# Stick-breaking scores in a hybrid attention layer: two query blocks on the two halves of the array's rows

## The chip, the cores and the metric

The kernel runs on one core of a Trainium2 chip. The core has TensorE (PE in the profile; its weight loads have a row of their own, PEld), VectorE (DVE), ScalarE (ACT), GpSimd (POOL), and SyncE (SP), whose queue issues nearly all of this kernel's DMAs. The metric is the device time of one execution in microseconds. All times below are microseconds unless marked ns.

## The reference, cut to what matters

The layer has two attention branches. The change is in the first, stick-breaking attention with 8 heads of 64 dimensions, 2048 real positions and 16 meta positions:

```python
for blk in range(L // BLOCK):                       # 128 queries at a time
    z = einsum('bqhd,bkhd->bhqk', q[:, q0:end], k[:, :end]) * scale
    mask = (s[None, :] < t[:, None]) & valid[None, :end]
    log_beta = log_sigmoid(z)
    log_1m = where(mask, log_beta - z, 0.0)
    rev = cumsum(log_1m, axis=3, reverse=True)
    suffix = concatenate([rev[..., 1:], zeros_like(rev[..., :1])], -1)
    w = where(mask, exp(log_beta + suffix), 0.0)
    outs.append(einsum('bhqk,bkhd->bqhd', w, v[:, :end]))
```

Everything is float32. Around it stand an RMS norm, one large input projection, the sliding-window branch, gates, two branch projections, an output projection and a final norm.

## The kernel before, in words

**Precision.** TensorE multiplies in a reduced float32 format here, so each float32 operand is split into a high part and a low part. A projection takes three products (high·high, low·high, high·low); these are the three matmuls at line 454 (`gemm`).

**Order of positions.** Sequences are reversed, so the suffix product of the reference becomes a running product, and each query block looks at keys to its right. The sequence is cut into four groups `g` of 512 positions. The program runs in two halves, first groups 2 and 3, then 0 and 1. In each half come projections, the sliding-window stage, and then the stick-breaking stage `stick(groups, bp)`.

**The stick-breaking stage.** A step is `(h, g, n, j)`: head `h`, query group `g`, key chunk `n`, query block `j` of four. Query block `j` against chunk `n` covers 512 keys that start on the block's own diagonal. In the last chunk the keys run out, and blocks 0 to 3 cover 512, 400, 272 and 144 columns, the last 16 of them the meta keys. Block 0 has no room for these 16 in its bank and puts them into another bank, `zm`.

- `row` (from line 899) makes the scores of a step: two matmuls at line 916 into one of two banks `z`. The contraction runs over all 128 rows of the array: the key tile `kt` holds the high keys of the head in rows 0 to 63 and the low keys in rows 64 to 127; `q1` holds high over low queries, `q2` low over high. Thus `q1` against `kt` gives high·high + low·low, and `q2` gives low·high + high·low. Line 918 does the same for the 16 meta columns. ScalarE then writes the sigmoid (line 920) into a row buffer, and VectorE runs the product scan over it (line 930; in the first half GpSimd masks the diagonal block before it, line 925).
- `turn` transposes four 128x128 pieces of rows that are 5 or 6 steps old (`LT`) into one of two banks `t` (line 941); `evac_split` takes them out as a high part on ScalarE (line 119) and a low part on VectorE (line 120).
- `values` multiplies these by the values (line 967), two steps after their `turn`.

`load_kv` and `load_q` fetch the keys, values and queries of a head over SP's queue. The key tile has two buffers, the row buffer twelve.

**Order of the work.** The order on TensorE is written out by hand: `weave` runs one step of three matmuls of a gate projection (line 454), and then as much of the stick-breaking generator as the costs that it yields allow. The generator yields estimates in us, 0.45 for the two score matmuls, 0.43 for a `turn`, 0.43 for a `values`. On the other engines and on SP's queue a planner decides the order beforehand; on the chip each engine runs its own list in order.

One more place matters as a comparison: `meta_cols` (line 475) transposes a tile of 16 rows, so that its matmul uses only a strip of the array's rows. It happens a few times in the first 320 us.

Of the kernel before, what the change touches and what calls it, by code (L numbers as in the profile page):

```python
# [7 lines left out]
F32 = mybir.dt.float32  # L8
# [8 lines left out]
P = 128  # L17
# [31 lines left out]
def tile_kernel(ctx, tc, x, xt, meta, metat, gain, w_in, w_sb, w_sw, w_out, sinks, fgain,  # L49
# [8 lines left out]
    def DMA(dst, src):  # L58
        nc.sync.dma_start(*(t.bitcast(F32) if t.dtype == F32R else t for t in (dst, src)))
# [788 lines left out]
    def stick(groups, bp):  # L848
        kt, vc = {}, {}
        rows_of = {}  # L850
        lt = LT[groups[0] == 0]
        KW = ((4 - groups[0]) * GT + P)
        for tag, shape, n in (("q1", [P, GT], 2), ("q2", [P, GT], 2), ("v", [P, 4, P], 5), ("wh", [P, GT], 3), ("wl", [P, GT], 3),
                              ("k", [P, KW], 2)):
# [16 lines left out]
        def load_kv(h, g):  # L871

            p, a = divmod(h, 2)
            r = slice(64 * a, 64 * a + 64)
            if h not in kt:
                kt[h] = bp.tile([P, KW], F32R, tag="k", name="kt", bufs=2)
            for c in range(g, 4):
                if (h, c) in vc:
                    continue
                c0 = (c - groups[0]) * GT  # L880
                cs = slice(c0, c0 + GT + (NM if c == 3 else 0))
                DMA(kt[h][0:64, cs], kd[p][c][0][r])
                DMA(kt[h][64:128, cs], kd[p][c][1][r])
                v = vc[h, c] = bp.tile([P, 4, P], F32R, tag="v", name="vc", bufs=5)
                DMA(v, vd[p][c][a])

# [9 lines left out]

        state = {}

        def row(h, g, n, j):

            if n == j == 0:
                load_kv(h, g)
                state[h, g] = {"q": load_q(h, g), "last": {}}
            st = state[h, g]
            last = st["last"]
            b0 = 4 * (g + n) + j
            nb = min(4, NB - b0)
            end = b0 + nb == NB
            w = nb * P + (NM if end and nb < 4 else 0)
            k0 = (b0 - 4 * groups[0]) * P  # L910
            own = end and nb == 4
            z = ps("z")
            zm = ps("zm") if own else None
            for t, qt in enumerate(st["q"]):
                lq = qt[:, j * P:(j + 1) * P]
                T.matmul(z[:, :w], lhsT=lq, rhs=kt[h][:, k0:k0 + w], start=t == 0, stop=t == 1)  # L916
                if own:
                    T.matmul(zm[:, :NM], lhsT=lq, rhs=kt[h][:, k0 + w:k0 + w + NM], start=t == 0, stop=t == 1)
            r = bp.tile([P, RW], F32, tag="row", name="row", bufs=12)
            A.activation(r[:, :w], z[:, :w], AF.Sigmoid, scale=-1.0)  # L920
            if own:
                A.activation(r[:, w:w + NM], zm[:, :NM], AF.Sigmoid, scale=-1.0)
                w += NM
            if n == 0 and mask is None:
                G.affine_select(out=r[:, :P], in_=r[:, :P], pattern=[[1, P]], compare_op=ALU.is_ge,  # L925
                                fill=1.0, base=-1, channel_multiplier=-1)
            if n == 0 and mask is not None:
                V.tensor_tensor_scan(r[:, :w], r[:, :w], mask[:, :w], 1.0, op0=ALU.mult, op1=ALU.max)
            else:
                V.tensor_tensor_scan(r[:, :w], r[:, :w], r[:, :w], last[j] if n else 1.0, op0=ALU.mult, op1=ALU.min)  # L930
            last[j] = r[:, w - 1:w]
            rows_of[h, g, n, j] = r
# [45 lines left out]
        turned = []  # L978
        for s in range(n + lt + 3):
            if s < n:  # L980
                row(*steps[s])
                yield 0.45 if s >= lt else 1.31
            t = s - lt
            if 0 <= t < n:
                turn(*steps[t])
                turned.append(s)
                yield 0.43
                if sum(steps[t][1:3]) == steps[t][3] == 3:
                    turn_meta(*steps[t][:2])
# [331 lines left out]
    for half, groups in enumerate(halves):  # L1321
# [168 lines left out]
```

## Time and profile before

| | |
|---|---|
| time, median of 3 runs | 2111.91 (2111.11 to 2116.18) |
| the profiled execution's own time | 2112.16 |
| its span | 2110.4 |
| PE busy | 2094.4 (99%) |
| PEld busy | 1755.2 (83%) |
| DVE busy | 1479.1 (70%) |
| ACT busy | 1058.8 (50%) |
| POOL busy | 300.1 (14%) |
| score matmuls, line 916, first to last start | 374.2 to 1599.5, in two stretches |

In a row of the timeline the first two numbers are the start and the duration; for a merged row (x2, x4) the duration covers all of them. Matmuls are pipelined, so a matmul's duration is longer than the distance to the next start; what a matmul costs is read from the distance between starts. A group row gives busy time, mean ns of one, then the engine's idle time just before the group and what ended it.

### The profile page before, as it was taken

Reading aid. Unit: us, or ns where it says so; the run is one execution under the profiler, and the core shown is the slowest. Engines: PE = TensorE matmul, PEld = TensorE weight load, DVE = VectorE, ACT = ScalarE, POOL = GpSimd, SP = SyncE. Lnnn points to the kernel's source line nnn. Section 1 sums busy time; section 2 is a strip of 40 time slices with the busy share of each in tenths; the row PEclk is TensorE's granted clock in tenths of the full one; section 3 lists DMA queues with packets and bytes.
Section 4 is the critical chain, followed back from the end, with each engine's and each line's share of the span. In section 5 each row is a group of like instructions: output and inputs, shape, how many; then the busy total and the mean of one; then the engine's idle time right before and its main releaser. Section 6 shows DMA issues by size and latency. Waiting matters only on the chain.

```text
span 2110.4 us, 30845 instructions
## 1 busy us (share of the span) xinstructions
PE 2094.4 (99%) x10695; PEld 1755.2 (83%) x10695; DVE 1479.1 (70%) x2375; ACT 1058.8 (50%) x2438; POOL 300.1 (14%) x484
## 2 busy tenths in 40 slices
PE   9999999999999999999999999999999999999998
PEld 7888888888878888888888888888888888788887
DVE  7897986888878554887738888877774456564553
ACT  6677774555646335777735555555553202221131
POOL 2133444211000000232310000000000232000000
PEclk9999999999999999999999999999999999999999
DMA  9955545766449674435455344343424996568532
GB/s 337 324 174 193 191 168 181 238 194 200 139 142 338 232 256 155 152 136 178 137 172 153 123 126 127 118 125 95 123 88 142 360 323 203 181 232 309 160 100 90
DMA packets 169580, 391.07 MB, mean 185 GB/s; under 512 B 23601, under 2 KB 27697, under 8 KB 169425
## 3 DMA queue, kind: packets, MB, share of 16 engines
q1 hardware_dynamic: 169136, 388.84, 54.9%
q8 instruction: 85, 1.39, 0.3%
q14 instruction: 71, 0.57, 0.1%
q10 hardware_dynamic: 288, 0.27, 0.0%
HBM read 241.68 MB, written 145.18 MB: 183 GB/s over the span
## 4 chain that ended last, share of the span: by engine, by line
PE 91%; DVE 3%; ACT 3%; DMA 2%; issue 1%; SPq 0%; ACTq 0%; DVEq 0%
PE ps_g L454 39%; PE ps_o L967 6%; PE ps_z L916 6%; PE ps_t L941 6%; PE ps_z L754 3%; PE ps_o L810 2%; PE ps_g L252 1%; PE ps_g L253 1%; PE ps_g L251 1%; PE ps_z L252 1%; PE ps_z L251 1%; PE ps_z L253 1%; PE ps_t L252 1%; PE ps_t L253 1%; PE ps_t L251 1%; PE ps_t L788 1%
## 5 line engine op out<-in xcount | busy, mean ns | idle before, releaser
L454 PE MATMUL ps_g<-xh,wh 128*128 128x512 f32 x1296 | 532.1, 411 | 0.8 <-DVE tmp L675 0.5
L454 PE MATMUL ps_g<-xl,wh 128*128 128x512 f32 x1296 | 507.6, 392 | 0.4 <-DVE xl L1169 0.3
L454 PE MATMUL ps_g<-xh,wl 128*128 128x512 f32 x1296 | 507.7, 392 | 0.0
L930 DVE TENSOR_TENSOR_SCAN row<-row 128x512 f32<-128x512 f32 (+4 forms) x256 | 297.1, 1161 | 91.9 <-ACT row L920 39.5
L454 PEld LDWEIGHTS ps_g<-xh,wl 128*128 128x128 f32 x1296 | 243.3, 188 | 54.4 <-DVE wl L1217 0.4
L920 ACT ACTIVATE row<-ps_z 128x512 f32<-128x512 f32 (+1 forms) x320 | 172.4, 539 | 213.5 <-PE ps_z L916 192.3
L454 PEld LDWEIGHTS ps_g<-xh,wh 128*128 128x128 f32 x1296 | 244.3, 188 | 41.4 <-ACT xh L1168 1.0
L454 PEld LDWEIGHTS ps_g<-xl,wh 128*128 128x128 f32 x1296 | 244.8, 189 | 37.8 <-DVE xl L1169 1.7
L119 ACT ACTIVATE wth<-ps_t 128x512 fp32r<-128x512 f32 (+1 forms) x320 | 170.7, 533 | 76.3 <-PE ps_t L941 75.2
L120 DVE SCALAR_TENSOR_TENSOR wtl<-ps_t,wth 128x512 fp32r<-128x512 f32 (+1 forms) x320 | 188.9, 590 | 25.3 <-ACT wth L119 24.8
L916 PE MATMUL ps_z<-kt,q 128*128 128x512 f32 (+3 forms) x640 | 185.3, 369 | 0.0
L941 PE MATMUL ps_t<-ident,row 128*128 128x128 f32 x1088 | 171.7, 273 | 0.1
L941 PEld LDWEIGHTS ps_t<-ident,row 128*128 128x128 f32 x1088 | 134.7, 140 | 34.0 <-DVE wtl L120 1.3
L916 PEld LDWEIGHTS ps_z<-kt,q 128*128 128x128 f32 x640 | 117.9, 188 | 23.5
L967 PE MATMUL ps_o<-wth,vc 128*128 128x512 f32 (+1 forms) x320 | 130.2, 407 | 0.0
L967 PE MATMUL ps_o<-wtl,vc 128*128 128x512 f32 (+1 forms) x320 | 116.3, 363 | 0.0
L762 ACT ACTIVATE sc<-sc,nm 128x129 f32<-128x129 f32 x256 | 100.0, 393 | 27.9 <-DVE nm L760 26.9
L115 POOL TENSOR_SCALAR wh<-raw 128x1024 fp32r<-128x1024 f32 (+1 forms) x47 | 52.8, 1124 | 354.0 <-PE ps_g L454 143.4
L610 ACT ACTIVATE tmp<-ps_g 128x512 f32<-128x512 f32 x84 | 50.3, 598 | 74.1 <-PE ps_g L454 67.0
L925 POOL TENSOR_SCALAR_AFFINE_SELECT row<-row 128x128 f32<-128x128 f32 x64 | 20.4, 318 | 468.2 <-ACT row L920 441.0
L290 ACT CAST ringl<-gt 128x512 fp32r<-128x512 f32 x32 | 19.9, 622 | 129.0 <-DVE gt L288 127.1
L794 POOL TENSOR_SCALAR_AFFINE_SELECT pm<-pl 64x256 fp32r<-64x256 f32 x128 | 74.3, 580 | 37.3 <-DVE pl L120 31.9
(441 smaller groups left out, 4130.1 us busy)
## 6 DMA issues: line engine op xcount, KB each, us to landing
wh<-h_in_w_in SPq DMA_DIRECT2D x66, 512.0 KB, 3.7
wl<-l_in_w_in SPq DMA_DIRECT2D x66, 512.0 KB, 4.9
h_in_w_in<-wh SPq DMA_DIRECT2D x50, 512.0 KB, 3.3
l_in_w_in<-wl SPq DMA_DIRECT2D x50, 512.0 KB, 3.5
raw<-in_w_in SPq DMA_DIRECT2D x49, 512.0 KB, 5.3
q<-qd SPq DMA_DIRECT2D x128, 128.0 KB, 3.3
vc<-vd SPq DMA_DIRECT2D x48, 256.0 KB, 3.1
kd<-tmp SPq DMA_DIRECT2D x32, 256.0 KB, 3.3
```

The source lines that it names most:

```text
L119: A.activation(h, acc, AF.Copy, scale=scale)
L120: V.scalar_tensor_tensor(l, acc, scale, f32(h), op0=ALU.mult, op1=ALU.subtract)
L251: T.matmul(acc, lhsT=wh[:, k, :], rhs=h, start=k == 0, stop=False)
L252: T.matmul(acc, lhsT=wh[:, k, :], rhs=l, start=False, stop=False)
L454: T.matmul(acc, lhsT=a[:, k, :], rhs=b[:, k, :], start=k == i == 0, stop=k == KT - 1 and i == 2)
L762: A.activation(sc[:, hh, :], sc[:, hh, :], AF.Exp, bias=nm[:, hh:hh + 1], accum_out=den[:, hh:hh + 1])
L794: G.affine_select(out=pm[to, :, c], in_=full[r, :, c], pattern=[[0, 4], [sign, HB]], compare_op=ALU.is_ge, fill=0.0, base=n - 1, channel_m ...
L916: T.matmul(z[:, :w], lhsT=lq, rhs=kt[h][:, k0:k0 + w], start=t == 0, stop=t == 1)
L920: A.activation(r[:, :w], z[:, :w], AF.Sigmoid, scale=-1.0)
L930: V.tensor_tensor_scan(r[:, :w], r[:, :w], r[:, :w], last[j] if n else 1.0, op0=ALU.mult, op1=ALU.min)
L941: T.transpose(tr[:, j * P:(j + 1) * P], rows_of[h, g, n - (j > i), j][:, k0:k0 + P], ident)
L967: T.matmul(o[:, :n], lhsT=v, rhs=r, start=first and r is wh, stop=last)
```

## The change

Two query blocks of a head, `j` and `j + 1`, are now multiplied together. One uses rows 0 to 63 of the array and the other rows 64 to 127, each with a contraction over 64 rows, and each into its own `z` bank. There are three rounds: high queries on high keys, low queries on high keys, high queries on low keys. The product low·low is no longer made for these blocks. For this the keys are kept in two tiles per head: `kh` has the high keys in both halves of its rows, `kl` the low keys in both halves. `q1` and `q2` stay as they are, and are read in halves.

Where the second block has 256 columns or fewer (blocks 2 and 3 of the last chunk), and for the 16 meta columns, full-height matmuls remain: `q1` on `kh`, then `q1` on `kl`.

The new helper `span(g, n, j)` holds the arithmetic that stood in `row`: the first key column of a block, its width, and whether its 16 meta columns stand apart.

The key tiles take four buffers where there were two, and four DMAs per chunk where there were two. The second half has eleven row buffers instead of twelve, a reserved piece of on-chip memory is set to 1024 bytes per partition, and the cost estimates of the generator become 0.72 for a pair.

```diff
-                              ("k", [P, KW], 2)):
+                              ("k", [P, KW], 4)):
...
-                kt[h] = bp.tile([P, KW], F32R, tag="k", name="kt", bufs=2)
+                kt[h] = [bp.tile([P, KW], F32R, tag="k", name="kt", bufs=4) for _ in range(2)]
...
-                DMA(kt[h][0:64, cs], kd[p][c][0][r])
-                DMA(kt[h][64:128, cs], kd[p][c][1][r])
+                for t, k in enumerate(kt[h]):
+                    for o in range(2):
+                        DMA(k[64 * o:64 * o + 64, cs], kd[p][c][t][r])
...
-            for t, qt in enumerate(st["q"]):
-                lq = qt[:, j * P:(j + 1) * P]
-                T.matmul(z[:, :w], lhsT=lq, rhs=kt[h][:, k0:k0 + w], start=t == 0, stop=t == 1)
-                if own:
-                    T.matmul(zm[:, :NM], lhsT=lq, rhs=kt[h][:, k0 + w:k0 + w + NM], start=t == 0, stop=t == 1)
-            r = bp.tile([P, RW], F32, tag="row", name="row", bufs=12)
...
+        def products(h, g, n, j):
...
+            st = state[h, g]
+            if j in st["z"]:
+                return 0
+            (q1, q2), (kh, kl) = st["q"], kt[h]
+            both = j % 2 == 0 and span(g, n, j + 1)[1] > 2 * P
+            js = (j, j + 1) if both else (j,)
+            zs_ = [ps("z") for _ in js]
+            if both:
+                lows, highs = slice(0, 64), slice(64, 128)
+                for i, (qa, qb, k) in enumerate(((q1, q2, kh), (q2, q1, kh), (q1, q2, kl))):
+                    for q, r, z, jj in ((qa, lows, zs_[0], j), (qb, highs, zs_[1], j + 1)):
+                        k0, w, _ = span(g, n, jj)
+                        T.matmul(z[:, :w], lhsT=q[r, jj * P:(jj + 1) * P], rhs=k[r, k0:k0 + w], start=i == 0, stop=i == 2)
+            else:
+                k0, w, _ = span(g, n, j)
+                for i, k in enumerate((kh, kl)):
+                    T.matmul(zs_[0][:, :w], lhsT=q1[:, j * P:(j + 1) * P], rhs=k[:, k0:k0 + w], start=i == 0, stop=i == 1)
+            for jj, z in zip(js, zs_):
+                k0, w, own = span(g, n, jj)
+                zm = None
                 if own:
+                    zm = ps("zm")
+                    for i, k in enumerate((kh, kl)):
+                        T.matmul(zm[:, :NM], lhsT=q1[:, jj * P:(jj + 1) * P], rhs=k[:, k0 + w:k0 + w + NM], start=i == 0, stop=i == 1)
+                st["z"][jj] = z, zm
+            return 0.72 if both else 0.45
...
+            z, zm = st["z"].pop(j)
+            r = bp.tile([P, RW], F32, tag="row", name="row", bufs=nrow)
...
+                cost = products(*steps[s])
                 row(*steps[s])
-                yield 0.45 if s >= lt else 1.31
+                if s < lt:
+                    yield 1.31
+                elif cost:
+                    yield cost
...
-            cost_sb = 8 * sum(4 * (4 - g) for g in groups) * 1.31 + 16 * 0.75 + LT[half] * 0.86
+            cost_sb = 8 * sum(4 * (4 - g) * 1.22 + 0.18 for g in groups) + 16 * 0.75 + LT[half] * 0.86
```

Sigmoid, scan, transposes, splits and the product with the values are the same operations on the same sizes.

More of the change, by code (lines that the diff above doesn't have):

```diff
@@ L852, in stick @@
         KW = ((4 - groups[0]) * GT + P)
+        nrow = 12 if groups[0] else 11
         for tag, shape, n in (("q1", [P, GT], 2), ("q2", [P, GT], 2), ("v", [P, 4, P], 5), ("wh", [P, GT], 3), ("wl", [P, GT], 3),
-                              ("k", [P, KW], 2)):
+                              ("k", [P, KW], 4)):
             for _ in range(n):
@@ L897, in stick, with span @@
         state = {}
[L899 to L905, printed above, removed]
+        def span(g, n, j):
             b0 = 4 * (g + n) + j
@@ L908, in row @@
             end = b0 + nb == NB
[L909 to L913, printed above, removed]
-            for t, qt in enumerate(st["q"]):
-                lq = qt[:, j * P:(j + 1) * P]
-                T.matmul(z[:, :w], lhsT=lq, rhs=kt[h][:, k0:k0 + w], start=t == 0, stop=t == 1)
-                if own:
-                    T.matmul(zm[:, :NM], lhsT=lq, rhs=kt[h][:, k0 + w:k0 + w + NM], start=t == 0, stop=t == 1)
@@ L919, in row @@
-            r = bp.tile([P, RW], F32, tag="row", name="row", bufs=12)
+            return (b0 - 4 * groups[0]) * P, nb * P + (NM if end and nb < 4 else 0), end and nb == 4
+        def products(h, g, n, j):
+            if n == j == 0:
+                load_kv(h, g)
+                state[h, g] = {"q": load_q(h, g), "last": {}, "z": {}}
+            st = state[h, g]
[18 more added lines that the diff above has]
+                zm = None
+                if own:
+                    zm = ps("zm")
[3 more added lines that the diff above has]
+            return 0.72 if both else 0.45
@@ L920, in row @@
+        def row(h, g, n, j):
+            st = state[h, g]
+            last = st["last"]
+            _, w, _ = span(g, n, j)
+            z, zm = st["z"].pop(j)
+            r = bp.tile([P, RW], F32, tag="row", name="row", bufs=nrow)
             A.activation(r[:, :w], z[:, :w], AF.Sigmoid, scale=-1.0)
-            if own:
+            if zm is not None:
                 A.activation(r[:, w:w + NM], zm[:, :NM], AF.Sigmoid, scale=-1.0)
@@ L1481 @@
     arrays = {k: np.ascontiguousarray(v) for k, v in arrays.items()}
-    nc = bacc.Bacc("TRN2", target_bir_lowering=False, num_devices=1)
+    nc = bacc.Bacc("TRN2", target_bir_lowering=False, num_devices=1, dynamic_dma_scratch_size=1024)
     args = [nc.dram_tensor(f"in_{k}", v.shape, mybir.dt.from_np(v.dtype), kind="ExternalInput").ap()
```

## The prediction

> **What bounds the kernel now.** I read the page's busy times first, then the stick-breaking stage by stretches, then single instructions in order of time.
>
> ```profile
> PE 2094.4 (99%) x10695; PEld 1755.2 (83%) x10695; DVE 1479.1 (70%) x2375; ACT 1058.8 (50%) x2438; POOL 300.1 (14%) x484
> ...
> L925 POOL TENSOR_SCALAR_AFFINE_SELECT row<-row 128x128 f32<-128x128 f32 x64 | 20.4, 318 | 468.2 <-ACT row L920 441.0
> ```
>
> ```profile
> 420.00:460.00 40.00, 40.00 (x227) 33.55 (x227) 33.68 (x44) 21.92 (x48) 5.54 (x3) 1.00 0.72 222
> 1200.00:1300.00 100.00, 100.00 (x544) 83.57 (x543) 82.96 (x102) 54.90 (x107) 3.80 (x13) 1.00 0.39 117
> ```
>
> The stretches list length, sum, PE, PEld, DVE, ACT, POOL, clock, DMA share and GB/s. In both stretches, one of each stick-breaking stage, PE is busy all the time (40.00 of 40.00, 100.00 of 100.00) at a granted clock of 1.00. So the time changes by what the change does to TensorE's stream, us for us, unless it opens a new wait. VectorE, at 83%, is next.
>
> What a score matmul costs is the distance between starts:
>
> ```profile
> 1249.72 0.52 PE L916 MATMUL ps_z<-kt,q 128*128 128x400 f32 x2
> 1250.09 0.60 PE L941 MATMUL ps_t<-ident,row 128*128 128x128 f32 x4
> ...
> 1255.56 0.62 PE L916 MATMUL ps_z<-kt,q 128*128 128x512 f32 x2
> 1256.03 0.60 PE L941 MATMUL ps_t<-ident,row 128*128 128x128 f32 x4
> ...
> 1257.62 0.62 PE L916 MATMUL ps_z<-kt,q 128*128 128x512 f32 x2
> ```
>
> ```profile
> 1255.80 0.59 PEld L941 LDWEIGHTS ps_t<-ident,row 128*128 128x128 f32 x4
> ```
>
> Two matmuls of 512 columns take 0.47, so 0.235 each; two of 400 take 0.37, so 0.185 each. The weight load of what follows starts at 1255.80, when the second score matmul begins, so weight loads lie under the running matmul. This holds although the transposes are of another type than the scores.
>
> **The rounds.** By the code there are 320 steps (8 heads; 4, 3, 2 and 1 chunks for the four groups; 4 blocks each). In a chunk that is not the last, blocks 0 and 1 and blocks 2 and 3 pair up with 512 columns each: 8 x 2 x (3 + 2 + 1 + 0) = 96 pairs. In the 32 last chunks (8 heads, 4 groups) blocks 0 and 1 pair up with 512 and 400 columns, and blocks 2 and 3 stay alone at two full-height matmuls, as now. So 128 pairs change. A (512, 512) pair costs 4 x 0.235 = 0.94 now, a (512, 400) pair 2 x 0.235 + 2 x 0.185 = 0.84. If the two halves run beside each other, three rounds take 3 x 0.235 = 0.705. That alone would give 96 x 0.235 + 32 x 0.135 = 26.9 less.
>
> **Changing the height of the matmuls.** Each pair stands in a stream of full-height matmuls. The trace has one place where the row height changes, the transposes of 16 rows:
>
> ```profile
> 83.67 0.39 PE L454 MATMUL ps_g<-xh,wl 128*128 128x512 f32 x1
> ...
> 83.98 0.13 PEld L475 LDWEIGHTS ps_t<-ident,ms 16*128 16x128 f32 x1 [0.35 <-issue]
> 83.99 0.23 PE L475 MATMUL ps_t<-ident,ms 16*128 16x16 f32 x1
> 84.14 0.19 PEld L454 LDWEIGHTS ps_g<-xh,wh 128*128 128x128 f32 x1
> ...
> 84.25 0.19 PEld L454 LDWEIGHTS ps_g<-xl,wh 128*128 128x128 f32 x1
> 84.49 0.40 PE L454 MATMUL ps_g<-xl,wh 128*128 128x512 f32 x1
> ```
>
> ```profile
> 92.23 0.20 PEld L475 LDWEIGHTS ps_t<-ident,back 16*128 16x128 f32 x2 [0.35 <-issue]
> 92.23 0.29 PE L475 MATMUL ps_t<-ident,back 16*128 16x16 f32 x2
> 92.35 0.14 PEld L475 LDWEIGHTS ps_zm<-ident,ms 16*128 16x128 f32 x1
> ```
>
> The load for the 16 rows does not start with the matmul before it at 83.67, as at 1255.80, but at 83.98, some 0.08 after that matmul's columns have gone in (83.67 + 0.23 = 83.90, with the distance above). Nothing is named as its releaser. The load for the full-height matmul after it also waits (84.14), and that matmul begins to stream at 84.49 - 0.23 = 84.26, which is when the next load starts (84.25). From 83.90 to 84.26 is 0.36 for a matmul of 16 columns that itself takes some 0.02. So going to a part of the rows and back costs 0.34: twice the array runs empty, and twice a weight load lies bare. These rows are 16 high and not 64; I take them over, since nothing nearer exists. Below, a change of height could cost nothing if 64 rows need no emptying (lower end 0); above 0.34 nothing in the trace points.
>
> The Trainium skill's page "TensorEngine Tiling (Array Packing)", section Key Properties, says the same in words: changing the tiling mode, and not just the tile, drains the TensorE. It gives no price; by it every pair pays twice, as in the sum here, and it speaks against this change.
>
> **Skew inside a pair.** The second half's weights load after the first half's. Three loads in a row of 16-row matmuls are 0.06 apart (92.23, then the third at 92.35), the load at 84.14 is followed at 84.25, 0.11 later. So the second half trails by 0.06 to 0.11; I take the middle, 0.085. Later rounds load under the rounds before.
>
> **Sum on TensorE.** A (512, 512) pair: 0.34 + 0.705 + 0.085 = 1.13 against 0.94, 0.19 more, x 96 = 18.2. A (512, 400) pair: the trailing half ends after 0.085 + 2 x 0.235 + 0.185 = 0.74, so 1.08 against 0.84, 0.24 more, x 32 = 7.7. Together 25.9; with a skew of 0.06 it is 23, with 0.11 it is 29.
>
> The page "TensorE: Matmul & The Clock Gate", section Part 3, lets row tiles start some 4 ns apart; by that the skew would vanish and the sum would be about 10 less. The same section measured 3.07 times for four tiles instead of 4; by that the three rounds would take 0.705 x 4 / 3.07 = 0.92, nearly what four rounds take now, and the sum would be some 27 more, near the rival below with rounds a third longer. No run here shows either.
>
> **Meta columns.** Now two 16-column matmuls interleave with block 0's:
>
> ```profile
> 411.50 0.39 PE L916 MATMUL ps_z<-kt,q 128*128 128x512 f32 x1
> ...
> 412.10 0.47 PE L454 MATMUL ps_g<-xh,wh 128*128 128x512 f32 x1
> 412.41 0.39 PE L454 MATMUL ps_g<-xl,wh 128*128 128x512 f32 x1
> ```
>
> From 411.50 to 412.10 is 0.60, 0.13 more than 0.47, and the next matmul takes 0.31 instead of 0.23: 0.21 together. Afterwards they come full-height behind the pair, two short matmuls with a bare load each, about 0.21 to 0.24. 32 times 0 to 0.03: 0.5.
>
> **Keys over SP's queue.** Key loads double, 96 more of about 0.55 each on the queue; nothing else moves through it in larger number. Where is that late? Only at the start of a stage, when the first keys and queries are fetched while a gate covers them. The second half:
>
> ```profile
> 1095.80 1.13 SPq L59 DMA_DIRECT2D kt<-kd  x2
> ...
> 1104.31 1.77 SPq L59 DMA_DIRECT2D q<-qd  x3
> ...
> 1110.98 0.53 SPq L59 DMA_DIRECT2D wh<-h_in_w_in  x1
> ```
>
> ```profile
> 1111.53 0.62 PE L916 MATMUL ps_z<-kt,q 128*128 128x512 f32 x2
> ...
> 1133.37 0.39 PE L454 MATMUL ps_g<-xh,wh 128*128 128x512 f32 x1
> ```
>
> ```profile
> q<-qd SPq DMA_DIRECT2D x128, 128.0 KB, 3.3
> ```
>
> Six more key loads ahead of the first queries move their last issue from 1106.08 to about 1109.4; landing 3.3 later is 1112.7, 1.2 after the first score needs them. Other stores change places too, so 0 to 1.2. The first half has two more ahead of its first queries, 0 to 1.1; for both I take 0.5. The weights issued at 1110.98 slip by eight key loads, 4.5; the gate tile that uses them begins at 1133.37, the seventeenth gate step counted from the last one before 1111.53, so some 14 us of cover remain even with a landing of several us. Later heads are fetched a head ahead; without that cover each would pay its extra loads, 2.2 in the first half and 4.4 in the second, 53 in all.
>
> **Order on ScalarE and VectorE.** Both blocks' scores end together, and the planner's list now has two sigmoids, two scans and then two splits where they alternated.
>
> ```profile
> 1258.34 0.60 ACT L920 ACTIVATE row<-ps_z 128x512 f32<-128x512 f32 x1 [0.97 <-PE ps_z L916]
> ```
>
> ```profile
> 1259.34 1.22 DVE L930 TENSOR_TENSOR_SCAN row<-row 128x512 f32<-128x512 f32 x1 [0.26 <-POOL row L925]
> 1260.48 0.67 DVE L120 SCALAR_TENSOR_TENSOR wtl<-ps_t,wth 128x512 fp32r<-128x512 f32 x1
> ```
>
> Both `z` banks are free 2 x 0.60 after the pair, well before the next pair. But the split that frees a `t` bank ends 0.60 + 0.4 + 2 x 1.22 + 0.67 = 4.1 after the pair (0.4 is 1259.34 less the sigmoid's end), instead of 2.9. TensorE wants that bank two steps later, 2 x 2.06 = 4.1 after it (scores start at 1255.56 and 1257.62), 4.3 with the longer pair. So nearly all of a slack of 1.2 goes; where GpSimd masks first (318 ns; 24 pairs of the first half), up to 0.3 may be lost each, 7 in all. I take 2, from 0 to 8. The queue behind such a wait is TensorE's whole stream.
>
> One row buffer less and the reserved memory: I cost them at nothing. A row is read up to 8 steps after it is written in the second half, and eleven buffers leave two spare, as in the first half now.
>
> **Forecast.** 25.9 + 0.5 + 0.5 + 2 = 28.9. The profiled execution took 2112.16 (0.25 above the median of 2111.91), so 2141.1, say 2141, 1.4% slower. Its own range: 23 + 0 to 29 + 0.5 + 2.3 + 8, 2135 to 2152.
>
> **Rivals.**
>
> *No emptying at 64 rows: faster.* It decides at one place, a round trip of the height. Without it the rounds gain 26.9, less the skew, 96 x 0.085 + 32 x 0.035 = 9.3, so 17.6 over 128 pairs: below 0.14 per round trip the kernel is faster. At 0 it takes 2094.5 (2085 without skew). For it: the rows show 16 high, once with three in a row, never 64. Against: the load before 83.98 waits although nothing releases it, and the return costs too. 0.21.
>
> *A wash*: a round trip near 0.14, between 0.09 and 0.19, 2106 to 2118. 0.07.
>
> *The halves do not run, or not fully, beside each other.* The trace holds no two matmuls on different rows, so nothing shows that they do. If they overlap, but each round is a third longer than 0.235, the rounds take 0.94, 128 x 0.235 = 30 more, 2171; 0.05. If they do not overlap at all, six half-height matmuls take 1.41 instead of four at 0.94: 96 x 0.47 + 32 x (3 x 0.42 - 0.84 = 0.42) = 58.6, 2171 without round trips, and 128 x 0.34 = 43.5 more with them, 2214; 0.09, half of it for each.
>
> *TensorE waits for VectorE's split* at most of the 128 pairs, some 0.3 each on top of the forecast: 38, 2179. Against it: VectorE's share of 83% leaves 17%. 0.04.
>
> The forecast keeps 0.54. Slower by over 0.3% (6 us, about what a measurement can tell from no change): 0.54 + 0.14 + 0.04 + 0.01 = 0.73; faster 0.21; within 0.06. The range goes from 2094, which keeps the upper part of the faster case, to 2180, which leaves out only the serial case with round trips.
>
> **What would show it.** The first weight load of a pair stands some 0.1 after the stream of the matmul before it, and so does the load after the pair; the two matmuls of a round start 0.06 to 0.11 apart, and rounds follow at 0.235. Distances from a pair's first start to the next full-height start show 1.1 (forecast), 0.75 (no emptying) or 1.4 and more (serial). PE's waits stay near zero; a wait of `ps_t` for the split at line 120 would be the last rival. It goes wrong above all if 64 rows do not behave like 16.

## The result, and the profile after

The changed kernel takes 2149.68 (median of 4 runs, 2146.81 to 2150.89) against 2111.91 before (2111.11 to 2116.18). The ratio is 1.0173, with a 95% interval of 1.0155 to 1.0190: 1.7% slower, 37.8 us. The forecast was 2141, with 2135 to 2152 as its own range.

The profiled executions took 2146.81 after and 2112.16 before, so 34.7 of the difference can be read from the two traces.

The page of the kernel after, busy times first, then groups of instructions:

```profile
PE 2122.9 (99%) x10951; PEld 1716.0 (80%) x10951; DVE 1485.0 (69%) x2375; ACT 1052.7 (49%) x2438; POOL 325.6 (15%) x484
...
L968 PE MATMUL ps_t<-ident,row 128*128 128x128 f32 x1088 | 172.8, 274 | 3.7 <-DVE wtl L120 3.6
...
L925 PE MATMUL ps_z<-kt,q 64*128 64x512 f32 (+1 forms) x768 | 124.4, 420 | 1.0 <-DMA q<-qd 1.0
...
L952 POOL TENSOR_SCALAR_AFFINE_SELECT row<-row 128x128 f32<-128x128 f32 x64 | 45.5, 711 | 463.0 <-ACT row L947 435.3
```

There are 256 more matmuls in all: 768 of 64 rows in 128 pairs, six each, where there were four of 128 rows. PE is still busy 99% of the span, and its wait for the split at line 120 is 3.6 in the whole execution. TensorE is the bound before and after; it has more to do per step.

The same two stretches as in the prediction, with the same columns:

```profile
420.00:460.00 40.00, 40.00 (x236) 31.14 (x235) 32.36 (x44) 21.23 (x48) 6.88 (x4) 1.00 0.64 194
1200.00:1300.00 100.00, 99.74 (x559) 73.65 (x558) 78.54 (x98) 51.22 (x104) 8.66 (x12) 1.00 0.39 122
```

PE has no idle time to speak of (40.00 of 40.00, 99.74 of 100.00), and the granted clock is 1.00. VectorE has 98 instructions in the 100 us where it had 102, and its busy time falls from 82.96 to 78.54: the same work has become sparser. The busy time of the weight loads falls too, from 83.57 to 73.65, though there are more of them (558 against 543). A part of that is only that the loads of the two halves lie over each other, as shown below.

Where a pair loses its time is seen around one of them, all engines, in order of time:

```profile
1257.19 0.39 PE L454 MATMUL ps_g<-xh,wl 128*128 128x512 f32 x1
1257.51 0.53 PEld L925 LDWEIGHTS ps_z<-kt,q 64*128 64x128 f32 x6 [0.36 <-issue]
1257.51 0.96 PE L925 MATMUL ps_z<-kt,q 64*128 64x512 f32 x6
1258.40 0.42 PEld L968 LDWEIGHTS ps_t<-ident,row 128*128 128x128 f32 x4 [0.36 <-DVE wtl L120]
```

The columns of the matmul at 1257.19 have gone in at 1257.42 (0.23 later, the distance between starts). The pair's first weight load begins at 1257.51, 0.09 after that. The first load of the transposes begins at 1258.40. Its 0.36 is put down to line 120, but loads behind a pair stand like this wherever nothing is late; it is the change of the height again, under another name. Over the 66 to 96 pairs in which the single records are complete the medians are: 0.09 until the first load, 0.107 for that load, 0.231 from round to round, 0.095 from the end of the last round's columns to the load behind the pair, and 0.11 for this load. Without the three rounds that is 0.40 for each stay at 64 rows.

What the two kinds of pair cost can be read in the order of PE alone, here with a (512, 512) pair and a (512, 400) pair that has meta columns:

```profile
1298.79 0.96 PE L925 MATMUL ps_z<-kt,q 64*128 64x512 f32 x6
1299.68 0.50 PE L454 MATMUL ps_g<-xh,wh 128*128 128x512 f32 x1
1300.01 0.40 PE L454 MATMUL ps_g<-xl,wh 128*128 128x512 f32 x1
...
1302.84 0.96 PE L925 MATMUL ps_z<-kt,q 64*128 64x512 f32 x6
1303.72 0.39 PE L936 MATMUL ps_zm<-kt,q 128*128 128x16 f32 x2
1303.97 0.49 PE L454 MATMUL ps_g<-xh,wh 128*128 128x512 f32 x1
1304.29 0.40 PE L454 MATMUL ps_g<-xl,wh 128*128 128x512 f32 x1
```

The record behind a pair begins with its bare load, so the stream is back at 1300.01 - 0.23 = 1299.78. With 1298.79 - 0.09 = 1298.70 as the end of the columns before, the pair took 1.08; the median is 1.10, against 2 x 0.463 = 0.93 for the four full-height matmuls before. That is 0.170 x 96 = 16.3. The second kind with its meta columns takes 1.33 against 0.688 + 0.375 = 1.063, so 0.267 x 32 = 8.5. Together 24.8 of the 34.7. Some 1.9 lies at the starts of the two stages, nearly all of it in the first, where the first scores wait for queries. That leaves 8.0, and they divide by stage, if one reads how much later the same matmuls start than in the kernel before. The first stage gets 12.5 longer, and 7.0 of that are its pairs (16 and 16 of the two kinds) and 1.7 its start, which leaves 3.8. The second gets 21.9 longer, with 17.9 for its pairs (80 and 16) and 0.2 for its start, which leaves another 3.8. What lies outside the stages adds 0.4; in it are 3.4 from 633.35 on at a granted clock of 0.50, where the kernel before has 1.00. The 3.8 and 3.8 are mostly waits of TensorE:

```profile
PEld ps_z L925 <- issue: 35.4, 97, 1.0
...
PEld ps_t L968 <- DVE wtl L120: 9.2, 17, 3.0
...
PEld ps_o L994 <- ACT tmp L998: 4.6, 13, 0.7
```

```profile
PE ps_t L968 <- DVE wtl L120: 3.6, 4, 2.8
PE ps_o L994 <- ACT tmp L998: 1.8, 4, 0.5
...
PE ps_z L925 <- DMA q<-qd: 1.0, 2, 0.7
```

These are the waits after (us in total, times, longest), of the weight loads and of the matmuls. The first row is the change of the height: 97 times some 0.36, no releaser. Of the 17 at line 968, 11 are more of those 0.36. PE's own wait there is 3.6; 3.4 of it lies in the first stage, and 2.8 is one single wait. One row each of VectorE, GpSimd and TensorE around it:

```profile
498.73 5.08 DVE L957 TENSOR_TENSOR_SCAN row<-row 128x400 f32<-128x400 f32 x2 [2.11 <-ACT row L947]
499.77 2.92 POOL L116 TENSOR_TENSOR wl<-raw,wh 128x1024 fp32r<-128x1024 f32 x1
504.78 0.66 PE L968 MATMUL ps_t<-ident,row 128*128 128x128 f32 x4 [2.77 <-DVE wtl L120]
```

Two scans, of 528 and 400 columns, stand ahead of two splits and take 5.08 together while GpSimd works on a weight tile beside them (line 116); on average such scans take 1.38 and 1.12. In the kernel before, the same work of GpSimd meets one scan of 272 columns, which takes 1.85 where 0.97 is the average, and TensorE does not wait.

The 13 at line 994 are waits of 0.2 or 0.7 for ScalarE's copy of the output bank at line 998, none of them a change of height; 12 lie in the second stage. So the first stage's 3.8 are nearly all the split, and the second's mostly the copy.

### The profile page after: what moved, and what is told of

It reads as the page before. It is cut to its first block, busy times and chain, and to the rows that moved or that the text cites. A ratio compares the mean times of both kernels' runs of the same rounds, so it can differ in the third digit from the quotient of the medians.

```text
span 2145.1 us, 31435 instructions
## 1 busy us (share of the span) xinstructions
PE 2122.9 (99%) x10951; PEld 1716.0 (80%) x10951; DVE 1485.0 (69%) x2375; ACT 1052.7 (49%) x2438; POOL 325.6 (15%) x484
## 4 chain that ended last, share of the span: by engine, by line
PE 90%; DVE 3%; ACT 2%; DMA 2%; issue 1%; SPq 0%; ACTq 0%; DVEq 0%
PE ps_g L454 38%; PE ps_o L994 6%; PE ps_t L968 6%; PE ps_z L925 5%; PE ps_z L754 3%; PE ps_o L810 2%; PE ps_z L454 2%; PE ps_g L252 1%; PE ps_g L253 1%; PE ps_g L251 1%; PE ps_z L252 1%; PE ps_z L251 1%; PE ps_z L253 1%; PE ps_t L252 1%; PE ps_t L251 1%; PE ps_t L253 1%
## 5 line engine op out<-in xcount | busy, mean ns | idle before, releaser
L454 PE MATMUL ps_g<-xh,wh 128*128 128x512 f32 x1296 | 541.5, 418 | 1.2 <-ACT xh L1199 0.8
L957 DVE TENSOR_TENSOR_SCAN row<-row 128x512 f32<-128x512 f32 (+4 forms) x256 | 290.7, 1159 | 119.4 <-ACT row L947 76.3
L947 ACT ACTIVATE row<-ps_z 128x512 f32<-128x512 f32 (+1 forms) x320 | 158.1, 536 | 197.3 <-PE ps_z L925 161.8
L120 DVE SCALAR_TENSOR_TENSOR wtl<-ps_t,wth 128x512 fp32r<-128x512 f32 (+1 forms) x320 | 183.2, 597 | 25.4 <-ACT wth L119 24.5
L925 PE MATMUL ps_z<-kt,q 64*128 64x512 f32 (+1 forms) x768 | 124.4, 420 | 1.0 <-DMA q<-qd 1.0
L952 POOL TENSOR_SCALAR_AFFINE_SELECT row<-row 128x128 f32<-128x128 f32 x64 | 45.5, 711 | 463.0 <-ACT row L947 435.3
L925 PEld LDWEIGHTS ps_z<-kt,q 64*128 64x128 f32 x768 | 64.0, 184 | 49.5 <-issue 35.4
L955 DVE TENSOR_TENSOR_SCAN row<-row,mask 128x512 f32<-128x512 f32 (+2 forms) x64 | 65.8, 1061 | 24.2 <-ACT row L947 23.8
L747 POOL COPY sc<-skb 128x4 f32<-128x4 f32 x64 | 20.2, 321 | 407.3 <-PE ps_t L788 220.3
```

The costliest lines, as they stand in the source:

```text
L120: V.scalar_tensor_tensor(l, acc, scale, f32(h), op0=ALU.mult, op1=ALU.subtract)
L454: T.matmul(acc, lhsT=a[:, k, :], rhs=b[:, k, :], start=k == i == 0, stop=k == KT - 1 and i == 2)
L925: T.matmul(z[:, :w], lhsT=q[r, jj * P:(jj + 1) * P], rhs=k[r, k0:k0 + w], start=i == 0, stop=i == 2)
```

## The experiments

The theory: TensorE is the bound; a pair costs 0.40 for the change of the height and three rounds of 0.23 with both halves beside each other; the rest is a loss of slack between the engines. The rivals are that the halves overlap only in part, that the pair order or the doubled keys cost the time and not the height, and that the waits alone do. Differences to the kernel before are taken in the same group of runs. Those to after go across groups, in which the kernel before itself differs by up to 1.3.

### Taking the change apart

**The pairs kept, but at full height.** The order of the work, the keys and the pairs are those of after; only the matmuls use all rows again.

```diff
-                for i, (qa, qb, k) in enumerate(((q1, q2, kh), (q2, q1, kh), (q1, q2, kl))):
-                    for q, r, z, jj in ((qa, lows, zs_[0], j), (qb, highs, zs_[1], j + 1)):
-                        k0, w, _ = span(g, n, jj)
-                        T.matmul(z[:, :w], lhsT=q[r, jj * P:(jj + 1) * P], rhs=k[r, k0:k0 + w], start=i == 0, stop=i == 2)
+                for jj, z in zip(js, zs_):
+                    k0, w, _ = span(g, n, jj)
+                    for i, k in enumerate((kh, kl)):
+                        T.matmul(z[:, :w], lhsT=q1[:, jj * P:(jj + 1) * P], rhs=k[:, k0:k0 + w], start=i == 0, stop=i == 1)
```

> Theory: the loss of 38 us is the emptying of the array and the bare weight loads at each change of row height (25 us), and the rest stalls behind the new order on ScalarE and VectorE and at the stage starts. With the pairs left in place but made of full-height matmuls (two per block, high and low keys) the heights never change, so 2112 + 2 for the starts + 5 to 12 for the stalls: 2119 to 2126. Rival: the pairing itself (both banks at once, grouped lists, doubled key loads) is the cost and the heights are cheap: 2140 or more.

Measured: 2121.49 (2120.94 to 2125.36), ratio 1.0043 (1.0028 to 1.0058). So 8.7 of the 37.8 have nothing to do with the half height (5.9 to 12.3 by the interval). Some 28 to 29 (2149.68 - 2121.49 = 28.2, or 37.8 - 8.7 = 29.1) go with the three rounds and the changes of height together. The two waits of the weight loads are there too, where no height changes (the lines of the code stand one higher):

```profile
PEld ps_t L967 <- DVE wtl L120: 6.6, 8, 3.0
PEld ps_o L993 <- ACT tmp L997: 4.6, 13, 0.7
```

So these waits come with the pairs and not with the height.

**The keys alone.** Here no pair is made, each block has its two full-height matmuls in its own step; what stays of the change is the two key tiles, the DMAs for them, the row buffers and the helper.

```diff
-            both = j % 2 == 0 and span(g, n, j + 1)[1] > 2 * P
+            both = False
...
-            cost_sb = 8 * sum(4 * (4 - g) * 1.22 + 0.18 for g in groups) + 16 * 0.75 + LT[half] * 0.86
+            cost_sb = 8 * sum(4 * (4 - g) for g in groups) * 1.31 + 16 * 0.75 + LT[half] * 0.86
```

> No pairs at all: every block alone with full-height matmuls on the two new key tiles, and the old cost estimates. Theory: doubled key loads, key tiles as high/high and low/low, eleven row buffers and the smaller reserve cost 0 to 2: 2112 to 2114. Rival: the key loads take a part of the 38 (queue or contention): 2120 or more.

Measured: 2114.84, just above what was expected, ratio 1.0007 (0.9997 to 1.0016), which cannot be told from before. The doubled keys are worth some 2 us by the medians, and at most 3.4 by the interval. The difference between the two kernels, 2121.49 - 2114.84 = 6.7, give or take some 4, is the price of making both blocks' scores in one step.

**The lists of VectorE and ScalarE by hand.** If those 6.7 come from the order that the planner gives to VectorE and ScalarE, an order by the sequence of the code should bring them back.

```diff
-            weave(tiles_by_tile(gts[few + 1:rest], groups), side, ratio)
+            with tc.manual_schedule(engines={mybir.EngineType.DVE}):
+                with tc.manual_schedule(engines={mybir.EngineType.Activation}):
+                    weave(tiles_by_tile(gts[few + 1:rest], groups), side, ratio)
```

> The changed kernel, with ScalarE's and VectorE's order in the stick-breaking stage as written in the program (sigmoid, scan, split, then the next block's) instead of the planner's two-by-two lists. Theory: the 7 us that TensorE stalls behind splits and behind the copy of the output bank come from the two-by-two lists, so 2141 to 2145. Rival: they come from the pair's latency itself and stay: 2148 to 2152.

Measured: 2143.52 (2142.57 to 2143.74), ratio 1.0142 (1.0127 to 1.0157), 6.2 less than after. VectorE's instructions, first after, then with the list by hand:

```profile
1254.51 2.57 DVE L957 TENSOR_TENSOR_SCAN row<-row 128x512 f32<-128x512 f32 x2 [1.24 <-POOL row L952]
1257.00 1.26 DVE L120 SCALAR_TENSOR_TENSOR wtl<-ps_t,wth 128x512 fp32r<-128x512 f32 x2
1259.14 2.46 DVE L957 TENSOR_TENSOR_SCAN row<-row 128x512 f32<-128x512 f32 x2 [0.88 <-ACT row L947]
```

```profile
1299.21 1.27 DVE L957 TENSOR_TENSOR_SCAN row<-row 128x512 f32<-128x512 f32 x1
1300.40 0.67 DVE L120 SCALAR_TENSOR_TENSOR wtl<-ps_t,wth 128x512 fp32r<-128x512 f32 x1
1301.01 1.32 DVE L957 TENSOR_TENSOR_SCAN row<-row 128x528 f32<-128x528 f32 x1
```

After, two scans stand ahead of two splits (x2 and x2), with idle time ahead of the scans; by hand they alternate. The waits of the weight loads with the lists by hand:

```profile
PEld ps_o L994 <- ACT tmp L998: 4.6, 13, 0.7
PEld ps_t L968 <- DVE wtl L120: 4.0, 11, 0.4
```

ScalarE's copy is waited for as in after (13 times, 4.6), so that wait does not come from the planner's lists; why it comes with the pairs is not shown. The wait for the split has gone from 9.2 to 4.0, and none of these is longer than 0.4, the change of the height. PE's own 3.6 are gone, with the single 2.8 among them. The two profiled executions differ by 4.2 (2146.81 - 2142.57), so what came back in them is mostly the wait for the split. But it is mostly one meeting of two scans with GpSimd's work, and not a small loss at each pair: the second stage, with 96 of the 128 pairs, is 21.7 longer than in the kernel before with the lists by hand, and 21.9 with the planner's.

**The same lists on the kernel before**, as a control: the same two lines around the same call.

> The kernel before with ScalarE's and VectorE's order in the stick-breaking stage as written in the program. Theory: nothing stalls there, so 2110 to 2113, and the 6 us that this order gave back with pairs belong to the pairs. Rival: the order by hand is better in any case: 2106.

Measured: 2112.47, ratio 1.0000 (0.9990 to 1.0009). The order by hand is worth nothing where blocks come one by one. The 6.2 come back only where there are pairs.

### The price of a change of height

**One short half-height matmul more, in the kernel before.** At the 128 places where after has a pair, a matmul of 16 columns over 64 rows goes ahead of the scores; the scores then overwrite what it wrote.

```diff
+            tick = slice(0, 64)
+            if j % 2 == 0 and (not end or j == 0):
+                T.matmul(z[:, :NM], lhsT=st["q"][0][tick, j * P:(j + 1) * P], rhs=kt[h][tick, k0:k0 + NM], start=True, stop=True)
```

> The kernel before, with one additional half-height matmul (64 rows, 16 columns, overwritten at once) ahead of the scores at the 128 places where the pairs stand. Theory: a change of height and back costs what the pairs showed, 0.36 to 0.42 each: 46 to 54 more, 2158 to 2166. Rival: only a bare weight load, 0.11 each: 2126.

**The same matmul over all 128 rows** (`tick = slice(0, P)`):

> The same additional 16-column matmul at the same 128 places, but full-height (128 rows). Theory: it costs a bare weight load and its 16 columns, 0.11 each as the meta columns show: 14 more, 2126. Rival: any small matmul there costs as much as the half-height one: 2158 or more.

Measured: 2163.46 with 64 rows, ratio 1.0237 (1.0217 to 1.0258), so 50.7 / 128 = 0.396 for each; 2128.36 with 128 rows, ratio 1.0072 (1.0049 to 1.0095), so 15.1 / 128 = 0.118 for each. The two kernels differ in nothing but the rows of that matmul, and the 64 rows cost 0.28 more. In the order of time, with 64 rows:

```profile
1251.38 0.39 PE L454 MATMUL ps_g<-xh,wl 128*128 128x512 f32 x1
...
1251.69 0.18 PEld L916 LDWEIGHTS ps_z<-kt,q 64*128 64x128 f32 x1 [0.36 <-issue]
1251.69 0.27 PE L916 MATMUL ps_z<-kt,q 64*128 64x16 f32 x1
1251.89 0.30 PEld L919 LDWEIGHTS ps_z<-kt,q 128*128 128x128 f32 x2
1251.90 0.73 PE L919 MATMUL ps_z<-kt,q 128*128 128x512 f32 x2
```

The reader sees the two gaps: columns gone in at 1251.38 + 0.23 = 1251.61, first load at 1251.69; bare load and 16 columns until some 1251.81, next load at 1251.89. So 64 rows behave as the 16 rows did that the prediction took over, and the rival without emptying falls. A matmul with next to no columns costs 0.12 at full height, its weight load, and 0.40 at half height. This bears out, with a price, what the Trainium skill's page "TensorEngine Tiling (Array Packing)" states in Key Properties, that changing the tiling mode drains the TensorE.

### The rounds and the halves

**Each pair's three rounds made twice.** The second time starts the sums afresh, so 384 rounds are added and no change of height.

```diff
-                for i, (qa, qb, k) in enumerate(((q1, q2, kh), (q2, q1, kh), (q1, q2, kl))):
+                three = ((q1, q2, kh), (q2, q1, kh), (q1, q2, kl))
+                for i, (qa, qb, k) in [*enumerate(three), *enumerate(three)]:
```

> The changed kernel with the three rounds of a pair made twice before the rows are left again (the second time overwrites the first). Theory: a pair has a fixed cost of 0.40 and 0.23 per round with both halves beside each other: 128 x 3 x 0.23 = 88 more, 2238. Rival A: the halves overlap only partly, so a round costs a third of the pair's 1.10: 140 more, 2290. Rival B: no overlap: 128 x 3 x 0.46 = 177 more, 2327.

Measured: 2237.45, ratio 1.0591 (1.0561 to 1.0622). That is 87.8 more than after, 0.229 for each round: two matmuls of 64 rows take the time of one of 128. Both rivals on the halves fall. The 3.07 times for four tiles that the Trainium skill's page "TensorE: Matmul & The Clock Gate" has in Part 3 would, by an estimate, have made a round some 0.30; two tiles of 64 rows with 512 columns don't show such a loss here.

**The halves one after the other in the order of the code:** three matmuls of the first half, then three of the second.

```diff
-                for i, (qa, qb, k) in enumerate(((q1, q2, kh), (q2, q1, kh), (q1, q2, kl))):
-                    for q, r, z, jj in ((qa, lows, zs_[0], j), (qb, highs, zs_[1], j + 1)):
-                        k0, w, _ = span(g, n, jj)
+                for a, (r, z, jj) in enumerate(((lows, zs_[0], j), (highs, zs_[1], j + 1))):
+                    k0, w, _ = span(g, n, jj)
+                    for i, (q, k) in enumerate(((st["q"][a], kh), (st["q"][1 - a], kh), (st["q"][a], kl))):
```

> The changed kernel with the six matmuls of a pair ordered by half: three on rows 0 to 63, then three on rows 64 to 127. Theory: matmuls start in program order, so only the third and fourth overlap: 0.46 more for 96 pairs and 0.31 more for 32, 54 more, 2204. Rival: TensorE starts the second half's matmuls ahead of the waiting first half's: 2150.

Measured: 2149.39, ratio 1.0174 (1.0145 to 1.0204), the same as after. My theory expected 2204 and fell; the rival was right. The pair in its trace:

```profile
1260.21 0.53 PEld L925 LDWEIGHTS ps_z<-kt,q 64*128 64x128 f32 x6 [0.36 <-issue]
1260.21 0.97 PE L925 MATMUL ps_z<-kt,q 64*128 64x512 f32 x6
```

Six loads in 0.53 and six matmuls in 0.97, against 0.53 and 0.96 in the alternating order. The order on TensorE is the code's, written by hand. The single records show the second half's first matmul 10 ns after the first half's, although two matmuls of the first half stand ahead of it in the order; in after it is 3 ns. The halves take their work as two streams, and the order in which the code names them hardly matters. That is what the Trainium skill's page "TensorEngine Tiling (Array Packing)" in Key Properties calls tiles that operate independently. Part 3 of the Trainium skill's page "TensorE: Matmul & The Clock Gate" calls matmuls strict in order, in start and end; by that this kernel would have been slower.

### Fewer changes of height

**Only the (512, 512) pairs.** The 32 pairs with 400 columns and meta columns go back to full height.

```diff
-            both = j % 2 == 0 and span(g, n, j + 1)[1] > 2 * P
+            both = j % 2 == 0 and span(g, n, j + 1)[1] == GT
```

> Pairs only where both blocks have 512 columns (96); the last chunk's blocks stay alone at full height. Theory: a (512, 400) pair with its meta columns loses 0.265, a (512, 512) pair 0.17 by the trace, so 32 x 0.265 = 8.5 come back: 2141. Rival: the height changes cost nothing that 32 fewer of them would show: 2150.

Measured: 2141.51 (2139.82 to 2142.15), ratio 1.0134 (1.0117 to 1.0151). The 32 pairs are worth 8.2, 0.26 each, as the distances between starts said (0.267).

**Four blocks in one stay**, on top of that: a stay then replaces eight matmuls by six rounds. The scores of blocks 2 and 3 are written over those of blocks 0 and 1, which the kernel leaves out, so it measures time and does not compute the layer.

```diff
-                for i, (qa, qb, k) in enumerate(((q1, q2, kh), (q2, q1, kh), (q1, q2, kl))):
-                    for q, r, z, jj in ((qa, lows, zs_[0], j), (qb, highs, zs_[1], j + 1)):
+                for d, (i, (qa, qb, k)) in [(d, t) for d in (0, 2) for t in enumerate(((q1, q2, kh), (q2, q1, kh), (q1, q2, kl)))]:
+                    for q, r, z, jj in ((qa, lows, zs_[0], j + d), (qb, highs, zs_[1], j + d + 1)):
...
-            return 0.72 if both else 0.45
+            if both:
+                st["z"][2], st["z"][3] = st["z"][0], st["z"][1]
+            return 1.2 if both else 0.45
```

> As the full pairs only, but the two pairs of a chunk are made in one stay at half height. For want of banks the second pair overwrites the first, so blocks 2 and 3 stand in for blocks 0 and 1 (their scores are left out); the amount of TensorE work is unchanged, only 48 of 96 round trips fall away. Theory: 48 x 0.40 = 19 less than with full pairs only, plus or minus 4 for stalls: 2118 to 2126, still not below 2112. Rival: the cost goes with the number of half-height matmuls and not with the stays: as full pairs only, 2141.

Measured: 2211.03 (2207.03 to 2216.56), ratio 1.0467 (1.0448 to 1.0486), some 90 more than expected. The waits of PE, then a moment in order of time:

```profile
PE ps_t L970 <- DVE wtl L120: 63.0, 57, 3.8
```

```profile
1305.40 1.66 PE L925 MATMUL ps_z<-kt,q 64*128 64x512 f32 x12
...
1307.73 3.63 DVE L959 TENSOR_TENSOR_SCAN row<-row 128x512 f32<-128x512 f32 x3 [2.06 <-ACT row L949]
```

The twelve half-height matmuls run as they should: 1.66 - 0.96 = 0.70 for three more rounds, 0.23 each. But with four rows ready at once the planner puts three scans in a row on VectorE, and TensorE waits 63.0 for the splits behind them. A further part is the clock: the granted clock is 0.990 on average over a span of 2214.8, which is an estimated 20 us more than at the 0.999 of the kernel before. The rival of the prediction in which TensorE waits for the split, which costs the changed kernel a few us, has become the main term here.

**The same with the lists of VectorE and ScalarE by hand:**

> Four rows a stay (blocks 2 and 3 again stand in for 0 and 1, their scores are left out) with ScalarE's and VectorE's order as written in the program. Theory: the 63 us that TensorE waited for splits there come from three scans in a row in the planner's list, so they go, and what is left is full pairs only, less 6 for the lists, less 48 x 0.40 = 19: 2113 to 2121. Rival: the banks held for four steps make the wait whatever the list's order: above 2150.

Measured: 2121.01 (2120.07 to 2123.09), ratio 1.0042 (1.0027 to 1.0057), 90 less than with the planner's lists, at the upper edge of what was expected. PE's waits for the split and for the copy are 2.5 each. Even so the kernel isn't faster than before, and for a real kernel of this kind four score banks would be needed where there are two. No version that I ran beats the kernel before.

## Why the prediction was right, step by step

**The bound.** TensorE was the bound and stayed it. Slower by 1.7% where 1.4% was forecast, within the likeliest case's own range of 2135 to 2152, in its upper part.

**The pairs on TensorE.** 26.4 with the meta columns were forecast, 24.8 are read from the distances between starts, and 28 to 29 is what undoing the half height gives. Why the last is larger is not shown; the intervals of the two measurements could hold the difference. Inside the sum two terms were mis-sized, and that they nearly cancel is luck. The round trip was put at 0.34 from matmuls of 16 rows; it is 0.40, by the trace of after and by the short matmul (0.396). The skew of 0.085 between the halves doesn't exist: their matmuls start 3 ns apart, and so do the weight loads of both (4 ns). So 0.425 was forecast beside the rounds and 0.40 measured. The 4 ns between row tiles that the Trainium skill's page "TensorE: Matmul & The Clock Gate" has in Part 3 agrees with these 3 ns. But the sum about 10 lower that the prediction drew from it was not measured, since the round trip was larger by nearly as much. The three rounds at 0.235 were right (0.231 in the trace, 0.229 by the doubled rounds).

**The meta columns** behind the pair were forecast with 0.5; they are part of the 8.5 for the second kind of pair (8.2 forecast with them).

**Keys and stage starts.** 0.5 was forecast with 2.3 as the upper end; the traces give some 1.9, and the keys without pairs some 2, which cannot be told from 0. The cover of later heads held: PE waits for queries twice in all, both times at the start of the first stage.

**Order on ScalarE and VectorE.** This is the term that was off in size: 2 was taken from a range of 0 to 8, and 7.6 is left in the two stages, near the edge of the range. The mechanism is only half right. Two scans ahead of two splits do eat the slack of 1.2, and the list by hand takes 6.2 back and does nothing to the kernel before. But the loss is not a few tenths at the pairs that GpSimd masks: in the second half, where these are, PE waits for a split once, for 0.3. It is mainly one wait of 2.8 in the first half, where two scans run beside GpSimd's work on a weight tile. The wait for ScalarE's copy of the output bank (line 998), 13 times and 4.6 in the row, was not in the prediction at all, and makes up most of the second half's share. The total fell inside the range only because this term was given up to 8: with 2 as its most the range would have ended at 2146. The prediction's sentence on GpSimd names the wrong half: by the code GpSimd masks the diagonal block in the second half, at 32 pairs, and in the first half a scan on VectorE does it. The text before the prediction has this the wrong way round too.

**The rivals.** No emptying: falls by the two short matmuls, 0.396 against 0.118. Its break-even of 0.14 per round trip was far below the 0.40. Halves beside each other only in part or not at all: falls by the doubled rounds. TensorE waits for the split at most pairs: not in after (3.6 of idle PE in all), but it does wait often in the kernel with four blocks per stay (57 times), where it is 63.0 of the 90 us that the lists by hand take back.

**What would show it.** The loads 0.09 after the stream, and rounds at 0.23, came as written; the two starts of a round did not. The distance from a pair's first start to the next full-height start did not either: it is 0.89 (1257.51 to 1258.40) and not 1.1. The pair's records begin 0.09 behind the stream, and the next record begins with its bare load of 0.11; only with these added is it the 1.1 that the sum meant.

## What to carry to other kernels

A matmul on half the rows, put into a stream of full-height ones, pays for the way in and out before it saves anything: here 0.40 for each stay against 0.23 for each round saved. A pair saves one round per stay and loses. By this sum a stay that saves two rounds gains next to nothing (0.46 against 0.40), and no run here shows a gain: with four blocks per stay, which saves two, the kernel took 2121.01 against 2112.37. So look for work that can remain at the smaller height much longer, and price a stay with one short matmul before building the rest. Work that is grouped on the bound engine also comes out grouped on the others: look at what the order of their lists does to the slack, and compare with an order by hand, before the loss is put down to the grouping itself. Then look whether the loss is many small waits or one large one.

## What the runs showed of the hardware that was not expected

The two halves of the rows are two streams for loads and matmuls alike. Two 64-row loads take the 0.107 of one, and three matmuls of one half ahead of three of the other cost nothing.

The mask on GpSimd became slower without any change to it: 711 ns each at line 952, where the kernel before has 318 ns for the same 64 instructions (line 925). What decides is whether VectorE scans beside it:

```profile
1254.19 0.29 POOL L952 TENSOR_SCALAR_AFFINE_SELECT row<-row 128x128 f32<-128x128 f32 x1 [3.35 <-ACT row L947]
1254.67 1.15 POOL L952 TENSOR_SCALAR_AFFINE_SELECT row<-row 128x128 f32<-128x128 f32 x1 [0.19 <-ACT row L947]
```

The first mask of this pair is done before the scans of 1254.51 begin and takes 0.29; the second runs beside them and takes 1.15. With the pairs at half height but the lists by hand the mean is 346 ns, and with full-height pairs and the planner's lists 720 ns, so it goes with the order of the lists and not with the height. The scans of 498.73 above, beside GpSimd's work on a weight tile, show that it slows VectorE as well.

A wait of TensorE can cost more than its length. PE in the kernel with four blocks per stay:

```profile
1297.23 0.39 PE L996 MATMUL ps_o<-wtl,vc 128*128 128x512 f32 x1
1300.78 1.12 PE L970 MATMUL ps_t<-ident,row 128*128 128x128 f32 x4 [3.16 <-DVE wtl L120]
1301.55 0.78 PE L454 MATMUL ps_g<-xh,wh 128*128 128x512 f32 x1
1302.12 0.63 PE L454 MATMUL ps_g<-xl,wh 128*128 128x512 f32 x1
1302.55 0.63 PE L454 MATMUL ps_g<-xh,wl 128*128 128x512 f32 x1
...
1304.38 0.39 PE L454 MATMUL ps_g<-xl,wh 128*128 128x512 f32 x1
1304.61 0.40 PE L454 MATMUL ps_g<-xh,wl 128*128 128x512 f32 x1
```

After 3.16 without work the matmuls start 0.43 apart (1302.12, 1302.55) where 0.23 is usual (1304.38, 1304.61), for some 2 us. The granted clock is 0.50 there, which accounts for it. The row has the columns of the stretches above (length, PE, PEld, DVE, ACT, POOL, clock, DMA share, GB/s):

```profile
1301.00:1303.00 2.00, 2.00 (x8) 1.71 (x8) 0.76 (x2) 0.60 (x1) 0.00 (x0) 0.50 0.00 0
```

Part 1 of the Trainium skill's page "TensorE: Matmul & The Clock Gate" names an idle window of about 3.4 us after which the clock is halved; a stretch of 3.16 was enough here. A shorter one can be enough, and need not be. The wait of 2.77 for the split stands both in the profile of after (504.78) and in that of the halves one after the other (504.22). The same six us, first of the latter, then of after:

```profile
504.00:510.00 6.00, 5.78 (x20) 5.04 (x21) 3.09 (x7) 1.38 (x3) 0.00 (x0) 0.50 0.80 273
504.00:510.00 6.00, 5.22 (x32) 4.08 (x33) 3.95 (x8) 2.26 (x5) 0.00 (x0) 1.00 0.82 246
```

So the same wait cost one execution some us more than the other. This may be why the other three executions of after take 2.6 to 4.1 longer than its profiled one, and why the lists by hand take 6.2 back and not 4.2; that is not shown.
